# Gate one-hots of a PEER decoder: one comparison for four tokens, products on GpSimd, and a split last write

## The chip, the cores and the metric

The kernel runs on one core of a Trainium2 chip. The metric is the time of one execution in device microseconds; the kernel before took 3640.11 us, the median of three runs (3639.72 to 3644.94).

## What is computed

A decoder trunk of two layers works on 512 tokens of 1024 features. Each layer has a hybrid mixer, a cross-attention and a PEER feed-forward part, each followed by a layer norm. Only the PEER part is touched:

```
v1, i1 = top_k(s1, 16); v2, i2 = top_k(s2, 16)          # per token and head, 128 keys each
sc, ci = top_k(v1[:, None] + v2[None, :], 16)
expert = i1[ci // 16] * 128 + i2[ci % 16]                # 8 heads x 16 = 128 experts per token
gate   = softmax(sc)
act    = gelu(sum_d x[t, d] * u[expert[t, e], d])
out[t] = sum_e gate[t, e] * act[t, e] * v[expert[t, e]]
```

## The kernel before, in words

For tokens 0 to 383 the PEER part is computed densely: all 128 x 128 experts, in 128 chunks of 128. For each chunk `u_chunk` makes the activations of the 384 tokens on TensorE (24 matmuls, lines 230 to 232, three passes of split floats) and `dense` later multiplies them by a gate matrix (`coef`), splits the result and multiplies it with the chunk of v (`v_block`). Tokens 384 to 511 are done by gathering rows of u and v with indirect DMAs on GpSimd's queue (`gathered`, L998), beside the dense part.

The gate matrix of one token is the sum over its 128 choices of gate times one-hot(first key) times one-hot(second key). `gate_rows` makes it as a matmul of two one-hot matrices with the 128 choices on the partitions. For a block of 128 tokens, TensorE transposes the keys and gates into a PSUM bank `pt` (L950, L954), ScalarE copies them to `st` (L951, L955), and then four tokens at a time (a quad) go through:

- VectorE, token by token: `o1 = (iota == key1) * gate` (L964) and `o2 = (iota == key2)` (L968); for three quads of sixteen ScalarE makes `o2` instead (L966, L970);
- TensorE: four matmuls into one bank (L973; the trace shows each as two passes);
- ScalarE: copy of the bank into a stage of 32 tokens (L974), which SP writes to the DRAM tensor `gates` once it is full (L977).

A layer has 3 blocks, 96 quads and 12 writes. The one-hots live in the arena `mid`, whose seven buffers of eight pages hold six quads and the block's columns. The dense part reads `gates` back in pieces of four chunks for all tokens (L1225).

Work is written as generators that are woven together in `body`; a scheduler then sets the order on each engine. Thirty chunks (`AHEAD`) of u are done ahead of the dense part: 20 with the routing, 3 (`EARLY`) at once, some woven into the gates' writing, and the last `LATE` after it. The split of a u chunk in this stage is a cast on ScalarE (L225) and a subtraction on VectorE (L226). DMAs of u, v and gates all go through SP's queue, in order.

Of the kernel before, what the change touches and what calls it, by code (L numbers as in the profile page):

```python
# [10 lines left out]
F32 = mybir.dt.float32  # L11
# [4 lines left out]
AF = mybir.ActivationFunctionType  # L16
OP = mybir.AluOpType
# [7 lines left out]
NK = 128  # L25
# [7 lines left out]
DT = 384  # L33
GT = 32
AHEAD = 30
QUERY = 20
EARLY = 3
LATE = 3
PF = 3
TAIL = 4  # L40
ROWS = 7
# [25 lines left out]
def weave(*streams):  # L67

    live = [[g, 0.0, t] for g, t in streams]
    while live:  # L70
        s = min(live, key=lambda s: s[1] / s[2])
        try:
            s[1] += next(s[0])
        except StopIteration:
            live.remove(s)
# [106 lines left out]
class K:  # L182
# [754 lines left out]
    def gate_rows(self, tb, ga, ef, dram, stages):  # L937

        nc = self.nc
        w = self.al((640,), F32, 1)  # L940
        f12 = w[:, 0:256].rearrange("p (a b) -> p a b", a=2)
        st = w[:, 256:640].rearrange("p (a b) -> p a b", a=3)
        pe = self.bank((128, 4, 128)).bitcast(I32)
        nc.vector.tensor_copy(pe[:, 0], ef[:, tb].rearrange("p h k -> p (h k)"))
        nc.vector.tensor_scalar(pe[:, 1], pe[:, 0], 7, None, op0=OP.logical_shift_right)
        nc.vector.tensor_scalar(pe[:, 2], pe[:, 0], 127, None, op0=OP.bitwise_and)
        nc.vector.tensor_copy(f12, pe[:, 1:3])
        pt = self.bank((128, 3, 128))
        for i in range(2):
            nc.tensor.transpose(pt[:, i, :], f12[:, i], self.ident)  # L950
        nc.scalar.copy(st[:, :2], pt[:, :2])  # L951
        if tb == 0:
            self.softmax(ga.rearrange("p t h k -> p (t h) k"))
        nc.tensor.transpose(pt[:, 2, :], ga[:, tb].rearrange("p h k -> p (h k)"), self.ident)  # L954
        nc.scalar.copy(st[:, 2], pt[:, 2])  # L955
        yield 2
        for g in range(128 // GT):
            stage = stages[:, g % 2]
            for q in range(0, GT, 4):
                t = g * GT + q  # L960
                o1, o2 = (self.al((4, NK), F32, 1) for _ in range(2))
                for k in range(4):
                    c1, c2, cg = (st[:, i, t + k:t + k + 1] for i in range(3))
                    nc.vector.tensor_scalar(o1[:, k], self.iota, c1, cg, op0=OP.is_equal, op1=OP.mult)  # L964
                    if t % 64 in (8, 24, 40):
                        nc.scalar.activation(o2[:, k], self.iota, AF.Abs, scale=-1.0, bias=c2)  # L966
                    else:
                        nc.vector.tensor_scalar(o2[:, k], self.iota, c2, None, op0=OP.is_equal)  # L968
                if t % 64 in (8, 24, 40):
                    nc.scalar.activation(o2, o2, AF.Relu, scale=-1.0, bias=1.0)  # L970
                bk = self.bank((128, 4, NK))
                for k in range(4):
                    nc.tensor.matmul(bk[:, k, :], o2[:, k, :], o1[:, k, :], start=True, stop=True)  # L973
                nc.scalar.copy(stage[:, :, q:q + 4], bk.rearrange("p t e -> p e t"))  # L974
                self.fr(o1, o2)
                yield 1.1
            nc.sync.dma_start(dram[:, tb * (128 // GT) + g], stage)  # L977
        self.fr(w)

    def gathered(self, l, tb, X, peer, gb, out):  # L980
# [98 lines left out]
    def body(self, out):  # L1079
# [19 lines left out]
        for l in range(L):  # L1099
# [15 lines left out]
            self.middle(self.F)  # L1115
            n = AHEAD - peer.c - LATE
            stages = self.al((2, NK, GT))
# [4 lines left out]
            weave(((peer.u_chunk() or 3.9 for _ in range(n - EARLY)), 3.9 * (n - EARLY)), (rows, 110))  # L1122
            for _ in range(LATE):
                peer.u_chunk()
# [247 lines left out]
```

## Time and profile before

| what | value |
|---|---|
| median of three runs | 3640.11 us |
| the profiled execution, its own time | 3637.7 us |
| its span on the core | 3636.0 us |
| TensorE busy | 3512.5 us (97%) |
| VectorE busy | 2694.8 us (74%) |
| ScalarE busy | 1425.0 us (39%) |
| GpSimd busy | 956.2 us (26%) |
| mean DMA rate | 205 GB/s |

Busy time is the time in which at least one instruction of the engine was running, as a share of the span. Matmul rows overlap, so TensorE's share says that it was occupied, not that it ran at its peak. An idle time is put down to the engine whose work ended it. Times in the rows are microseconds from the span's start, means of one instruction are nanoseconds.

### The profile page before, as it was taken

Reading aid. Unit: us, or ns where it says so; the run is one execution under the profiler, and the core shown is the slowest. Engines: PE = TensorE matmul, PEld = TensorE weight load, DVE = VectorE, ACT = ScalarE, POOL = GpSimd, SP = SyncE. Lnnn points to the kernel's source line nnn. Section 1 sums busy time; section 2 is a strip of 40 time slices with the busy share of each in tenths; the row PEclk is TensorE's granted clock in tenths of the full one; section 3 lists DMA queues with packets and bytes.
Section 4 is the critical chain, followed back from the end, with each engine's and each line's share of the span. In section 5 each row is a group of like instructions: output and inputs, shape, how many; then the busy total and the mean of one; then the engine's idle time right before and its main releaser. Section 6 shows DMA issues by size and latency. Waiting matters only on the chain. (4 is left out here: it accounts for less than half of the span.)

```text
span 3636.0 us, 50571 instructions
## 1 busy us (share of the span) xinstructions
PE 3512.5 (97%) x18546; PEld 3054.1 (84%) x18546; DVE 2694.8 (74%) x6206; ACT 1425.0 (39%) x2351; POOL 956.2 (26%) x629
## 2 busy tenths in 40 slices
PE   9999999898999999999999999998999999999998
PEld 6678888777899999998876788887779999999987
DVE  4675469997777777778746755699978777777787
ACT  5553332453333333334345533324533333333342
POOL 0110043002344444445101100430014444443450
PEclk9999999999999999999999999999999999999999
DMA  4142222347988888889612322313479888888894
GB/s 149 58 149 67 91 98 71 111 166 258 319 300 301 296 293 296 301 294 328 235 36 69 126 73 97 101 63 119 160 277 331 286 304 299 301 288 303 296 328 151
DMA packets 280297, 744.47 MB, mean 205 GB/s; under 512 B 21616, under 2 KB 120176, under 8 KB 276976
## 3 DMA queue, kind: packets, MB, share of 16 engines
q1 hardware_dynamic: 206320, 472.76, 37.9%
q0 software_dynamic: 73728, 268.47, 21.2%
q8 instruction: 146, 2.39, 0.3%
q14 instruction: 103, 0.84, 0.1%
HBM read 685.57 MB, written 55.57 MB: 204 GB/s over the span
## 5 line engine op out<-in xcount | busy, mean ns | idle before, releaser
L232 PE MATMUL bk<-parts 128*128 128x384 f32 (+1 forms) x3746 | 1353.7, 361 | 4.5 <-DVE parts L226 4.5
L231 PE MATMUL bk<-parts 128*128 128x384 f32 (+2 forms) x3752 | 1336.5, 356 | 2.6 <-DVE parts L226 2.4
L230 PE MATMUL bk<-parts 128*128 128x512 f32 (+1 forms) x3554 | 1280.1, 360 | 13.7 <-ACT parts L225 13.7
L226 DVE TENSOR_TENSOR parts<-plain,parts 128x1024 fp32r<-128x1024 f32 (+2 forms) x747 | 727.8, 983 | 424.5 <-issue 362.7
L225 ACT CAST parts<-plain 128x1024 fp32r<-128x1024 f32 (+2 forms) x787 | 656.4, 863 | 729.8 <-PE bk L231 636.2
L232 PEld LDWEIGHTS bk<-parts 128*128 128x128 f32 x3746 | 705.5, 188 | 74.7 <-DVE parts L226 7.7
L231 PEld LDWEIGHTS bk<-parts 128*128 128x128 f32 x3752 | 708.2, 189 | 67.6 <-DVE parts L226 3.3
L230 PEld LDWEIGHTS bk<-parts 128*128 128x128 f32 x3554 | 670.7, 189 | 77.1 <-ACT parts L225 14.3
L998 POOL DMA_INDIRECT mid<-peer_u,plain x256 | 372.9, 1457 | 916.2 <-DVE plain L1033 374.0
L998 POOL DMA_INDIRECT mid<-peer_v,plain x256 | 381.2, 1489 | 514.4 <-DVE mid L1021 386.4
L230 PE MATMUL bk<-parts,mid 128*128 128x512 f32 (+2 forms) x912 | 350.3, 387 | 11.2 <-ACT mid L225 7.8
L1215 ACT ACTIVATE plain<-bk 128x384 f32<-128x384 f32 x256 | 125.5, 490 | 582.5 <-PE bk L232 579.5
L1033 DVE SCALAR_TENSOR_TENSOR plain<-mid,plain 128x1024 f32<-128x1024 f32 x256 | 328.8, 1284 | 3.2
L231 PE MATMUL bk<-parts,mid 128*128 128x512 f32 (+2 forms) x912 | 326.6, 359 | 1.5 <-DVE parts L226 1.5
L1021 DVE SCALAR_TENSOR_TENSOR mid<-mid,plain 128x1024 f32<-128x1024 f32 x256 | 303.1, 1219 | 3.0 <-DMA mid<-peer_u,plain 3.0
L973 PE MATMUL bk<-mid 128*128 128x128 f32 x1536 | 282.5, 311 | 13.2 <-DVE mid L964 6.9
L973 PEld LDWEIGHTS bk<-mid 128*128 128x128 f32 x1536 | 219.5, 195 | 75.8 <-DVE mid L968 33.2
L232 PE MATMUL bk<-parts,mid 128*128 128x512 f32 (+2 forms) x720 | 253.1, 353 | 0.0
L964 DVE TENSOR_SCALAR mid<-iota,mid 128x128 f32<-128x128 f32 x768 | 245.8, 341 | 0.3 <-ACT mid L955 0.3
L225 ACT CAST mid<-plain 128x1024 fp32r<-128x1024 f32 x163 | 169.0, 1038 | 193.0 <-PE bk L232 84.7
L226 POOL TENSOR_TENSOR parts<-plain,parts 128x1024 fp32r<-128x1024 f32 x40 | 99.4, 2489 | 524.9 <-ACT parts L225 505.7
L230 PE MATMUL bk<-mid,parts 128*128 128x256 f32 (+1 forms) x798 | 237.0, 297 | 0.0
(237 smaller groups left out, 3834.5 us busy)
## 6 DMA issues: line engine op xcount, KB each, us to landing
plain<-peer_uT SPq DMA_DIRECT2D x256, 512.0 KB
plain<-peer_v SPq DMA_DIRECT2D x256, 512.0 KB
gates<-plain SPq DMA_DIRECT2D x24, 2048.0 KB
plain<-gates SPq DMA_DIRECT2D x64, 768.0 KB
plain<-w_in SPq DMA_DIRECT2D x44, 512.0 KB
plain<-xa_wkv SPq DMA_DIRECT2D x32, 512.0 KB
plain<-peer_wq SPq DMA_DIRECT2D x32, 512.0 KB
plain<-w_out SPq DMA_DIRECT2D x16, 512.0 KB
```

Source lines behind the costliest of these rows:

```text
L225: nc.scalar.copy(hi, src)
L226: return (eng or nc.vector).tensor_sub(lo, src, hi.bitcast(F32))
L230: nc.tensor.matmul(out, lt[0], rt[0], start=first, stop=False)
L231: nc.tensor.matmul(out, lt[0], rt[1], start=False, stop=False)
L232: nc.tensor.matmul(out, lt[1], rt[0], start=False, stop=last)
L964: nc.vector.tensor_scalar(o1[:, k], self.iota, c1, cg, op0=OP.is_equal, op1=OP.mult)
L973: nc.tensor.matmul(bk[:, k, :], o2[:, k, :], o1[:, k, :], start=True, stop=True)
L998: nc.gpsimd.indirect_dma_start(out=t, out_offset=None, in_=self.a[n], in_offset=bass.IndirectOffsetOnAxis(ap=ei[:, s:s + 1], axis=0))
L1021: nc.vector.scalar_tensor_tensor(u, u, 1.0, x, op0=OP.mult, op1=OP.mult, accum_out=act[:, s:s + 1])
L1033: nc.vector.scalar_tensor_tensor(acc, v, act[:, s:s + 1], acc, op0=OP.mult, op1=OP.add)
L1215: k.nc.scalar.activation(g, bk[:, :DT], AF.Gelu)
```

## The change

Per quad, one VectorE instruction compares both key columns, read straight from the PSUM bank `pt` by broadcast, with `iota` and writes both one-hots of four tokens (128 x 1024 elements). GpSimd multiplies the first one-hot by the gates. For two quads of eight ScalarE makes the second one-hot, and VectorE's instruction has 128 x 512 elements. `LATE` goes from 3 to 5. The last write of `gates` in a layer is issued as two: the columns of the first eight chunks, then the rest.

```diff
-LATE = 3
+LATE = 5
...
         for g in range(128 // GT):
             stage = stages[:, g % 2]
             for q in range(0, GT, 4):
                 t = g * GT + q
-                o1, o2 = (self.al((4, NK), F32, 1) for _ in range(2))
-                for k in range(4):
-                    c1, c2, cg = (st[:, i, t + k:t + k + 1] for i in range(3))
-                    nc.vector.tensor_scalar(o1[:, k], self.iota, c1, cg, op0=OP.is_equal, op1=OP.mult)
-                    if t % 64 in (8, 24, 40):
-                        nc.scalar.activation(o2[:, k], self.iota, AF.Abs, scale=-1.0, bias=c2)
-                    else:
-                        nc.vector.tensor_scalar(o2[:, k], self.iota, c2, None, op0=OP.is_equal)
-                if t % 64 in (8, 24, 40):
-                    nc.scalar.activation(o2, o2, AF.Relu, scale=-1.0, bias=1.0)
+                n = 1 if q % 16 == 8 else 2
+                o = self.al((2, 4, NK), F32, 1)
+                sh = [128, n, 4, NK]
+                nc.vector.tensor_tensor(o[:, :n], pt[:, :n, t:t + 4, None].to_broadcast(sh),
+                                        self.iota[:, None, None, :].to_broadcast(sh), op=OP.is_equal)
+                nc.gpsimd.tensor_mul(o[:, 0], o[:, 0], st[:, 2, t:t + 4, None].to_broadcast([128, 4, NK]))
+                if n == 1:
+                    for k in range(4):
+                        nc.scalar.activation(o[:, 1, k], self.iota, AF.Abs, scale=-1.0, bias=st[:, 1, t + k:t + k + 1])
+                    nc.scalar.activation(o[:, 1], o[:, 1], AF.Relu, scale=-1.0, bias=1.0)
                 bk = self.bank((128, 4, NK))
                 for k in range(4):
-                    nc.tensor.matmul(bk[:, k, :], o2[:, k, :], o1[:, k, :], start=True, stop=True)
+                    nc.tensor.matmul(bk[:, k, :], o[:, 1, k, :], o[:, 0, k, :], start=True, stop=True)
                 nc.scalar.copy(stage[:, :, q:q + 4], bk.rearrange("p t e -> p e t"))
-                self.fr(o1, o2)
+                self.fr(o)
                 yield 1.1
-            nc.sync.dma_start(dram[:, tb * (128 // GT) + g], stage)
+            at = tb * (128 // GT) + g
+
+            for a, b in ((0, NK),) if at + 1 < DT // GT else ((0, 8), (8, NK)):
+                nc.sync.dma_start(dram[:, at, a:b], stage[:, a:b])
```

In the changed kernel the compare stands at L965, the product at L967, the matmuls at L974, the copy at L975, the writes at L981, the gathers at L1002 and the reads of gates at L1229.

GpSimd's queue at the end of layer 0's gate stage (the `mid` buffers hold quads or gathered rows), first before:

```order
L226 TENSOR_TENSOR parts<-plain,mid_78 128x1024
L226 TENSOR_TENSOR parts<-plain,parts 128x1024 x7
L998 DMA mid_5556<-peer_u,plain 128x1024
L998 DMA mid_5560<-peer_u,plain 128x1024
L998 DMA mid_5561<-peer_u,plain 128x1024
```

and now:

```order
L967 TENSOR_TENSOR mid_5560<-mid_5560,mid_5562 128x512
L1002 DMA mid_5556<-peer_u,plain 128x1024
L967 TENSOR_TENSOR mid_5561<-mid_5561,mid_5562 128x512
L967 TENSOR_TENSOR mid_5559<-mid_5559,mid_5562 128x512
L1002 DMA mid_5560<-peer_u,plain 128x1024
L967 TENSOR_TENSOR mid_5557<-mid_5557,mid_5562 128x512
L967 TENSOR_TENSOR mid_5558<-mid_5558,mid_5562 128x512
L1002 DMA mid_5561<-peer_u,plain 128x1024
```

The first gather came straight after the last splits of the u chunks; now 96 products stand between, and two gathers stand ahead of the layer's last four and last two products.

SP's queue at the same place, with the queues each instruction waits for (a name with DMAHW is one of eight queues that DMAs take in turn), before:

```order
L977 DMA gates<-plain 128x4096 [waits DMAHW4_49,Activation_49]
L1178 DMA plain<-peer_v 128x1024 [waits DMAHW5_49,DMAHW1_49,DVE_49]
L1178 DMA plain<-peer_uT 128x1024
L1225 DMA plain<-gates 128x12x128 [waits DMAHW7_49,DMAHW4_49]
L1225 DMA plain<-gates 128x12x128
```

and now:

```order
L981 DMA gates<-plain 128x256 [waits DMAHW2_49,Activation_49]
L981 DMA gates<-plain 128x3840
L1182 DMA plain<-peer_v 128x1024 [waits DMAHW4_49]
L1182 DMA plain<-peer_uT 128x1024 [waits DVE_49]
L1229 DMA plain<-gates 128x12x128 [waits DMAHW6_49,DMAHW3_49,DMAHW2_49]
L1229 DMA plain<-gates 128x12x128
```

The small write takes queue 2 and the large one queue 3, and the first read of gates waits for both (queue 6 is its own), where it waited for the one write on queue 4 (queue 7 was its own).

TensorE's queue between two token blocks of layer 0, before:

```order
L973 MATMUL bk<-mid_5561 128x128 x4
L950 MATMUL bk<-ident,mid_5562 128x128 x2
L954 MATMUL bk<-ident,plain 128x128
L973 MATMUL bk<-mid_5557 128x128 x4
L973 MATMUL bk<-mid_5558 128x128 x4
```

and now:

```order
L974 MATMUL bk<-mid_5557 128x128 x4
L974 MATMUL bk<-mid_5558 128x128 x4
L950 MATMUL bk<-ident,mid_5559 128x128 x2
L954 MATMUL bk<-ident,plain 128x128
L974 MATMUL bk<-mid_5560 128x128 x4
L974 MATMUL bk<-mid_5561 128x128 x4
```

In both orders the next block's transposes stand behind all quads of the block before; what changed is what must follow them (a compare, and a product on GpSimd) before the next matmul can start.

## Rows read from the trace of the kernel before

**Rows 1.** The page's busy time, share of the span and instructions by engine.

```profile
PE 3512.5 (97%) x18546; PEld 3054.1 (84%) x18546; DVE 2694.8 (74%) x6206; ACT 1425.0 (39%) x2351; POOL 956.2 (26%) x629
```

**Rows 2.** Busy time by stretch, around the gate stage of layer 0.

```profile
core 0: us, PE busy (x) PEld busy (x) DVE busy (x) ACT busy (x) POOL busy (x), PEclk, DMA share, GB/s
681.10:739.50 58.40, 55.26 (x307) 45.13 (x307) 58.35 (x241) 36.57 (x72) 0.00 (x0) 0.97 0.35 140
853.50:869.40 15.90, 15.87 (x92) 15.55 (x90) 2.86 (x3) 3.87 (x6) 8.64 (x8) 1.00 0.93 350
869.40:878.10 8.70, 0.00 (x0) 0.00 (x0) 1.11 (x3) 0.52 (x2) 0.00 (x0) 0.69 1.11 341
```

**Rows 3.** L973's own view (ns min/median/max), and a row of TensorE's timeline.

```profile
L973 PE MATMUL bk<-mid x1536: 270/275/553, 689.8 to 2668.7; 128*128 128x128 f32 x192
...
726.33 0.38 PE L973 MATMUL bk<-mid 128*128 128x128 f32 x2
```

**Rows 4.** Timeline of VectorE at the start of layer 0's gate stage.

```profile
676.13 3.50 DVE L226 TENSOR_TENSOR parts<-plain,parts 128x1024 fp32r<-128x1024 f32 x3
...
683.01 2.63 DVE L968 TENSOR_SCALAR mid<-iota,mid 128x128 f32<-128x128 f32 x13
...
689.40 0.85 DVE L964 TENSOR_SCALAR mid<-iota,mid 128x128 f32<-128x128 f32 x3
```

**Rows 5.** VectorE by line and shape, 681.1 to 853.5 us: count, busy, mean, idle.

```profile
L964 DVE TENSOR_SCALAR mid<-iota,mid 128x128 f32<-128x128 f32 x384 | 123.6, 344 | 0.2 <-ACT mid L955 0.2
L968 DVE TENSOR_SCALAR mid<-iota,mid 128x128 f32<-128x128 f32 x312 | 86.8, 283 | 2.2 <-ACT mid L951 2.2
```

**Rows 6.** Timeline of TensorE, with its waits, at both layers' gate stages.

```profile
681.11 0.66 PE L950 MATMUL bk<-ident,mid 128*128 128x128 f32 x2 [7.22 <-DVE mid L947]
...
878.14 0.80 PE L230 MATMUL bk<-parts 128*128 128x512 f32 x1 [8.77 <-ACT parts L225]
...
2496.54 0.66 PE L950 MATMUL bk<-ident,mid 128*128 128x128 f32 x2 [7.22 <-DVE mid L947]
...
2689.89 0.79 PE L230 MATMUL bk<-parts 128*128 128x512 f32 x1 [4.92 <-ACT parts L225]
```

**Rows 7.** Timeline of GpSimd, and of VectorE beside it, in layer 0.

```profile
159.93 1.90 POOL L495 TENSOR_TENSOR plain<-plain 128x512 f32<-128x512 f32 x1 [5.45 <-PE bk L230]
...
220.27 1.04 POOL L495 TENSOR_TENSOR plain<-plain 128x512 f32<-128x512 f32 x1 [5.19 <-DVE plain L470]
...
221.05 0.69 DVE L577 SCALAR_TENSOR_TENSOR plain<-bk,plain 128x512 f32<-128x512 f32 x1 [0.85 <-ACT plain L576]
...
479.15 4.75 POOL L226 TENSOR_TENSOR mid<-plain,mid 128x1024 fp32r<-128x1024 f32 x2 [10.93 <-ACT mid L225]
```

**Rows 8.** GpSimd by line and shape, whole span.

```profile
L639 POOL TENSOR_TENSOR plain<-plain 128x512 f32<-128x512 f32 x4 | 5.1, 1285 | 2.0 <-DVE plain L638 2.0
```

**Rows 9.** ScalarE by line and shape, 681.1 to 853.5 us.

```profile
L974 ACT COPY plain<-bk 128x512 f32<-128x512 f32 x96 | 55.9, 585 | 56.6 <-PE bk L973 55.9
L966 ACT ACTIVATE mid<-iota,mid 128x128 f32<-128x128 f32 x72 | 27.1, 399 | 2.1 <-PE bk L973 1.6
```

**Rows 10.** Timeline of TensorE and ScalarE between the first two token blocks, layer 0.

```profile
741.33 0.41 PE L950 MATMUL bk<-ident,mid 128*128 128x128 f32 x2 [2.00 <-DVE mid L947]
...
741.78 0.37 ACT L951 COPY mid<-bk 128x256 f32<-128x256 f32 x1 [1.82 <-PE bk L950]
```

**Rows 11.** Timeline of GpSimd: the first gathers of layer 0 and layer 1.

```profile
845.20 9.71 POOL L998 DMA_INDIRECT mid<-peer_u,plain  x1 [200.29 <-PE bk L973]
...
2660.49 1.00 POOL L998 DMA_INDIRECT mid<-peer_u,plain  x1 [199.96 <-ACT plain L974]
```

**Rows 12.** Timeline of SP's queue and VectorE: last gates write, gates back.

```profile
854.04 0.33 SPq L977 DMA_DIRECT2D gates<-plain  x1
...
876.99 1.49 DVE L1236 TENSOR_TENSOR plain<-plain 128x384 f32<-128x384 f32 x3 [14.79 <-DMA plain<-gates]
...
2670.24 0.33 SPq L977 DMA_DIRECT2D gates<-plain  x1
```

## The prediction

> **What bounds the kernel now.** I read the page's busy shares first, then the stretches of the first layer, then VectorE, GpSimd and the queue waits inside the stretch that the change touches. Over the whole span TensorE is busy 97% [rows 1], so only a stage in which TensorE is not the pace can gain. The gate stage is one: from the first transposes of L950 to the last gate column it fills 172 us of layer 0, and in its first third VectorE is busy 58.35 of 58.40 us [rows 2]. TensorE's 55.26 us there are overstated, since matmul rows overlap: two passes of L973 together take 0.38 us where the median of one is 0.275 [rows 3], so they follow each other every 0.11 us, and the eight passes of four tokens need about 0.89 us. VectorE needs more. One L964 starts every 0.26 us (three in 0.85 us) and one L968 every 0.20 us (thirteen in 2.63 us) [rows 4], so four tokens cost 4 x 0.26 + 4 x 0.20 = 1.8 us. With 384 L964 and 312 L968 in the layer [rows 5] that is 162 us. The stage is VectorE's.
>
> Behind it TensorE runs late u chunks for 15.9 us (92 matmuls, 0.173 us each, so 4.15 us for a chunk of 24) and then stands still, in layer 0 for 8.77 us and in layer 1 for 4.92 us, until the first gates are back from DRAM and split [rows 2, 6]. From L950 to the first dense matmul it is 681.11 to 878.14 = 197.0 us in layer 0 and 2496.54 to 2689.89 = 193.4 us in layer 1 [rows 6]. The sum replaces these two stretches; the rest of the program keeps its order.
>
> **The change, part by part.** *Compares.* Four tokens now take one VectorE instruction of 128x1024 (72 of 96 quads a layer) or 128x512 (24 quads). No row shows this form. The nearest are three 128x1024 subtractions in 3.50 us, one every 1.17 us [rows 4], and a 128x512 with a PSUM operand at 0.69 us [rows 7], which starts the next about 0.6 us on. That gives 72 x 1.17 + 24 x 0.6 = 99 us a layer in place of 162, a mean of 1.0 us per quad. Bounds: 0.9 (the PSUM side no dearer) to 1.2 (every wait exposed); both stay under the next item, so neither is priced.
>
> *Products.* Each quad adds one GpSimd multiply of 128x512 with two different operands. The row of that kind is 1.285 us (L639) [rows 8]; two queued 128x1024 instructions with two operands took 4.75 us [rows 7], 2.375 each or 1.19 for each half. Between 1.19 and 1.285, near the row of the right size, I take one product every **1.25 us**. Bounds: 1.04 us, what GpSimd takes where both operands are one tensor [rows 7], and 1.90 us, what the same instruction took beside a VectorE subtraction with two SBUF operands [rows 7]. I stay at 1.25: the compare has one operand in PSUM, and beside such an instruction (L577, 0.69 us, from 221.05) GpSimd kept its 1.04 us [rows 7]. So GpSimd, at 1.25, becomes the pace, over VectorE at 1.0 and TensorE at 0.89.
>
> On elementwise work a rule speaks against this. The rows say 1.285 us on GpSimd against 0.69 us on VectorE. The Trainium skill, GPSIMD Engine Reference, section Engine selection, gives elementwise multiplies to VectorE because GpSimd is about twice as slow with two inputs; the ratio of these rows agrees. By that rule the product would stay on VectorE, a quad would cost 1.0 + 0.6 = 1.6 us there, and the result would be 3584 + 2 x 96 x 0.35 = 3651 us. The sum goes by the slower of two engines that work side by side, which the rule does not weigh.
>
> *ScalarE.* It forms 24 instead of 18 quads of the second one-hot. Its copies and absolute values were 55.9 + 27.1 us a layer [rows 9]; 6 x 4 more of 0.40 us add 10, and the closing passes stay small beside that. It stays under the 120 us that GpSimd needs, and works up to six buffers ahead: nothing.
>
> *Block boundaries.* The 32 quads of a token block end before the next block's transposes on TensorE, in both orders. Now three engines stand behind each other there: the last quad 0.95, transposes and wait 0.7, ScalarE's copy (0.37 us [rows 10]) with its hand-over 0.4, a compare 1.2: 3.3 us without a product, twice a layer, 6.6 us. TensorE's gap at that place in the kernel before was 2.00 us [rows 10], which is the lower bound; 5 us each is the upper.
>
> *Gathers on GpSimd's queue.* The first gathers now stand between the last six products: one ahead of four products, one ahead of two. The first gather of the program took 9.71 us; the first of layer 1 took 1.00 [rows 11], and with some 0.3 us to the next instruction I count 1.25 for an ordinary one. In the old order nothing waited for it. I charge 9.71 + 0.3 + 1.25 = 11.3 us in layer 0 and 2.5 us in layer 1. Bounds: 2.5 us, if the 9.71 does not come back, and 14 us.
>
> *Lead-in.* Before, the first L964 starts 8.3 us after L950 (689.40 [rows 4]). The split L226 now stands ahead of L852, and the first product needs a compare (1.2 us) behind L852: 8.8 us.
>
> *LATE 5.* Two chunks move out of the stage, where GpSimd's pace leaves TensorE idle anyway, to behind it. Six chunks then follow the last gate: 24.9 us. The gates' own path, from the issue of the last write to the first dense matmul, was 854.04 to 878.14 = 24.1 us in layer 0 (VectorE gets the gates at 876.99) and 19.7 us in layer 1 [rows 6, 12]; one more microsecond lies between the last pass and that issue. So 25.1 us in layer 0, 24.9 in layer 1: both standstills go, paid with 8.3 us of chunks each.
>
> *The write split in two.* In the built order the first gates read waits for two write queues, the small write's and the large one's, where it waited for one. So it comes no earlier: nothing, at best 0.2 us in layer 0.
>
> **Sum.** Layer 0: 8.8 lead-in + 96 x 1.25 = 120.0 + 6.6 + 11.3 + 1.1 (last quad) + 25.1 = 172.9 us against 197.0. Layer 1: 8.8 + 120.0 + 6.6 + 2.5 + 1.1 + 24.9 = 163.9 against 193.4. Saved: 24.1 + 29.5 = 53.6 us. The profiled execution's own time is 3637.7 us (span 3636.0), 2.4 us under the median 3640.1 of the runs shown; 3637.7 - 53.6 = **3584 us**.
>
> **The rivals.** *VectorE and GpSimd take turns* (slower). If the compare kept GpSimd from its operands as L226 did, a quad would cost 1.17 + 1.25 us (72 of them) or 0.6 + 1.25 (24), 2.28 on average, 99 us more per layer: 3584 + 198 = 3782. It decides from a pitch of 1.5 us, where the stage eats what it saves. For it: the 1.90 us row; against it: 1.04 us beside a PSUM operand [rows 7]. The Trainium skill, SBUF — State Buffer, section Who interferes with whom, states the lock between the two engines and excepts VectorE instructions with at most one SBUF input; the rows just named agree with both halves. Chance 0.07.
>
> *Products at 1.40 us*, by the broadcast operand or the hand-overs, which no row shows: 2 x 96 x 0.15 = 29 us, 3613. Chance 0.15.
>
> *Products near 1.04 us*: then the mean pace falls to about 1.08, where VectorE and TensorE hold it: 33 us less, 3551. Chance 0.10.
>
> *The DMA engines set the dense start.* They are at 0.93 and more behind the stage [rows 2], and gathers, gate writes, reads, v and u loads still meet there; 10 us a layer would give 3604. Against it: no u chunk needed there is loaded there, since the order has all of them issued in the stage. Chance 0.10.
>
> *The change does not do what it says*: for the split of the write it is already so in the sum.
>
> **How the numbers follow.** The forecast, at 0.58, has its own spread of some 10 us (boundary, first gather). The range, 3556 to 3614, holds it, the backlog and the 1.40 case, and leaves out the turn-taking (0.07), most of the fast products (0.07) and a tail beyond 1.40 (0.05). A measurement of this kernel tells a change from none at about 0.2%, 7 us. Only the turn-taking and mishaps beyond a pitch of 1.5 end slower: faster 0.92, same 0.02, slower 0.06.
>
> **What would show it.** In the profile of the changed kernel: GpSimd's multiply at about 1.28 us and one every 1.25; VectorE's compare at 1.2 us with idle time behind GpSimd; a GpSimd row of nearly 10 us among the last products of layer 0 alone, with TensorE idle beside it; GpSimd pauses of about 3 us at two places a layer; no wait of several microseconds before the first dense matmul. Wrong would be multiplies of 1.6 us and more, compares of 2 us, or TensorE still standing before the dense part.

## The result, and the profile after

The changed kernel took 3532.7 us (median of four runs) beside 3642.5 us for the kernel before: a ratio of 0.9704, 95% interval 0.9682 to 0.9727. It is faster, as forecast, by twice as much as forecast: the prediction was 3584, its range ended at 3556. The profiled execution's own time is 3532.14 us, its span 3530.4; all differences below are of spans, 3636.0 to 3530.4 = 105.6 us.

The page's busy times after, against [rows 1]:

```profile
PE 3417.4 (97%) x18546; PEld 3022.8 (86%) x18546; DVE 2570.0 (73%) x5006; ACT 1431.2 (41%) x2411; POOL 1136.0 (32%) x821
```

TensorE runs the same 18546 matmuls in 95 us less of occupied time, at the same 97%. The share says nothing; where TensorE was held by others, it is held for less.

The two new lines' own views (ns min/median/max; first and last start), where [rows 7, 8] had given the bounds:

```profile
L967 POOL TENSOR_TENSOR mid<-mid,mid x192: 1036/1039/1048, 692.4 to 2560.7; 128x512 f32<-128x512 f32 x192
...
L965 DVE TENSOR_TENSOR mid<-bk,iota x192: 674/1215/1225, 691.1 to 2555.8; 128x1024 f32<-128x1024 f32 x144, 128x512 f32<-128x512 f32 x48
```

The compare is as expected. The product is not: 1.04 us each time, none longer than 1.048, where 1.28 was expected.

GpSimd's timeline through layer 0's gate stage (start, duration of the merged row, count, and in brackets the idle time before it with what ended it), against [rows 11]:

```profile
692.39 32.11 POOL L967 TENSOR_TENSOR mid<-mid,mid 128x512 f32<-128x512 f32 x32 [46.42 <-DVE mid L965]
728.70 1.04 POOL L967 TENSOR_TENSOR mid<-mid,mid 128x512 f32<-128x512 f32 x1 [4.20 <-DVE mid L965]
729.89 22.00 POOL L967 TENSOR_TENSOR mid<-mid,mid 128x512 f32<-128x512 f32 x22 [0.16 <-DVE mid L965]
754.19 9.29 POOL L967 TENSOR_TENSOR mid<-mid,mid 128x512 f32<-128x512 f32 x9 [2.30 <-DVE mid L965]
767.69 1.04 POOL L967 TENSOR_TENSOR mid<-mid,mid 128x512 f32<-128x512 f32 x1 [4.21 <-DVE mid L965]
768.89 26.98 POOL L967 TENSOR_TENSOR mid<-mid,mid 128x512 f32<-128x512 f32 x27 [0.16 <-DVE mid L965]
797.04 1.11 POOL L1002 DMA_INDIRECT mid<-peer_u,plain  x1 [1.17 <-ACT plain L975]
798.18 2.04 POOL L967 TENSOR_TENSOR mid<-mid,mid 128x512 f32<-128x512 f32 x2
800.38 0.97 POOL L1002 DMA_INDIRECT mid<-peer_u,plain  x1 [0.16 <-POOL mid L967]
801.38 2.04 POOL L967 TENSOR_TENSOR mid<-mid,mid 128x512 f32<-128x512 f32 x2
```

GpSimd has no gap between its products: 32 of them in 32.11 us, a pause of 4.2 us at each block boundary, one of 2.30 us behind the one u chunk that is still woven in, and two gathers of about 1 us between the last products. All 96 products take 96.5 us.

VectorE has no gap between its compares either. Its timeline over the first block, and at the woven chunk:

```profile
691.09 32.03 DVE L965 TENSOR_TENSOR mid<-bk,iota 128x1024 f32<-128x1024 f32 x32 [0.78 <-ACT mid L955]
...
751.17 1.80 DVE L226 TENSOR_TENSOR parts<-plain,parts 128x1024 fp32r<-128x1024 f32 x1 [0.86 <-PE bk L231]
```

The next compare starts 1.13 us behind the start of a full one and 0.60 us behind that of a half one (128x512): one starts at 692.23 and, four quads later, one at 696.22. That is 1.00 us a quad, as on GpSimd: the two engines set the pace together.

TensorE's timeline at the same places, against [rows 6, 10], and the gates' return, against [rows 12]:

```profile
693.49 0.79 PE L974 MATMUL bk<-mid 128*128 128x128 f32 x2 [2.73 <-POOL mid L967]
...
729.79 4.55 PE L974 MATMUL bk<-mid 128*128 128x128 f32 x22 [2.80 <-POOL mid L967]
...
2440.73 0.66 PE L950 MATMUL bk<-ident,mid 128*128 128x128 f32 x2 [7.22 <-DVE mid L947]
...
2587.74 0.39 PE L230 MATMUL bk<-parts 128*128 128x512 f32 x1
```

```profile
805.33 0.80 SPq L981 DMA_DIRECT2D gates<-plain  x2
817.44 2.92 SPq L1229 DMA_DIRECT2D plain<-gates  x2
825.89 1.03 DVE L1240 TENSOR_TENSOR plain<-plain 128x384 f32<-128x384 f32 x2 [7.56 <-DMA plain<-gates]
```

The first dense matmul (L230, 128x512) of layer 1 starts with no wait before it, at 2587.74; in layer 0 it does so at 829.50. From L950 to it: 681.92 to 829.50 = 147.6 us in layer 0, and 147.0 in layer 1. That is 49.4 and 46.4 us less than [rows 6] give. Of the rest of the 105.6 us, 7.2 lie between the dense start of layer 0 and layer 1's L950 and 3.4 behind the dense start of layer 1; 0.8 us was lost ahead of layer 0's L950.

### The profile page after: what moved, and what is told of

Same layout as the page of the kernel before. It is cut to its first block, busy times and chain, and to the rows that moved or that the text cites. A ratio compares the mean times of both kernels' runs of the same rounds, so it can differ in the third digit from the quotient of the medians.

```text
span 3530.4 us, 49767 instructions
## 1 busy us (share of the span) xinstructions
PE 3417.4 (97%) x18546; PEld 3022.8 (86%) x18546; DVE 2570.0 (73%) x5006; ACT 1431.2 (41%) x2411; POOL 1136.0 (32%) x821
## 4 chain that ended last, share of the span: by engine, by line
PE 81%; DVE 12%; issue 3%; ACT 2%; POOL 1%; DMA 1%; DVEq 0%; SPq 0%; POOLq 0%; ACTq 0%
PE bk L230 24%; PE bk L231 23%; PE bk L232 23%; PE bk L974 5%; DVE bk L866 2%; DVE bk L860 1%; DVE plain L862 1%; PE bk L771 1%; DVE parts L226 1%; PE bk L742 1%; PE bk L572 1%; PE bk L528 1%; DVE plain L327 1%; DVE plain L858 1%; DVE plain L864 1%
## 5 line engine op out<-in xcount | busy, mean ns | idle before, releaser
L230 PE MATMUL bk<-parts 128*128 128x512 f32 (+1 forms) x3554 | 1276.1, 359 | 0.7 <-ACT parts L225 0.7
L226 DVE TENSOR_TENSOR parts<-plain,parts 128x1024 fp32r<-128x1024 f32 (+2 forms) x747 | 730.0, 985 | 445.4 <-issue 363.9
L230 PEld LDWEIGHTS bk<-parts 128*128 128x128 f32 x3554 | 669.0, 188 | 63.4 <-ACT parts L225 1.1
L1002 POOL DMA_INDIRECT mid<-peer_v,plain x256 | 377.4, 1474 | 494.4 <-DVE mid L1025 377.4
L1002 POOL DMA_INDIRECT mid<-peer_u,plain x256 | 363.9, 1421 | 530.6 <-DVE plain L1037 378.7
L230 PE MATMUL bk<-parts,mid 128*128 128x512 f32 (+2 forms) x912 | 349.5, 386 | 11.1 <-ACT mid L225 7.6
L226 POOL TENSOR_TENSOR parts<-plain,parts 128x1024 fp32r<-128x1024 f32 x40 | 99.4, 2490 | 526.6 <-ACT parts L225 507.8
L230 PE MATMUL bk<-mid,parts 128*128 128x256 f32 (+1 forms) x798 | 237.0, 297 | 0.0
L967 POOL TENSOR_TENSOR mid<-mid,mid 128x512 f32<-128x512 f32 x192 | 192.6, 1040 | 115.6 <-DVE mid L965 114.8
L232 PE MATMUL bk<-mid,parts 128*128 128x256 f32 (+1 forms) x798 | 228.9, 287 | 0.0
L230 PEld LDWEIGHTS bk<-parts,mid 128*128 128x128 f32 (+1 forms) x912 | 171.8, 189 | 56.6 <-issue 17.8
```

Source lines behind the costliest of these rows:

```text
L226: return (eng or nc.vector).tensor_sub(lo, src, hi.bitcast(F32))
L230: nc.tensor.matmul(out, lt[0], rt[0], start=first, stop=False)
L232: nc.tensor.matmul(out, lt[1], rt[0], start=False, stop=last)
L967: nc.gpsimd.tensor_mul(o[:, 0], o[:, 0], st[:, 2, t:t + 4, None].to_broadcast([128, 4, NK]))
L1002: nc.gpsimd.indirect_dma_start(out=t, out_offset=None, in_=self.a[n], in_offset=bass.IndirectOffsetOnAxis(ap=ei[:, s:s + 1], axis=0))
```

## The experiments

**1. What makes the product cheap.** Edit, against the changed kernel:

```diff
-nc.gpsimd.tensor_mul(o[:, 0], o[:, 0], st[:, 2, t:t + 4, None].to_broadcast([128, 4, NK]))
+nc.gpsimd.tensor_mul(o[:, 0], o[:, 0], w[:, 128:640].rearrange("p (a b) -> p a b", a=4))
```

> Only the second operand of GpSimd's product differs: 512 separate elements per partition (the block's key and gate columns as they lie) in place of the four gate columns broadcast. The gates are therefore not applied; the work and its order stay. Theory: the broadcast operand is what makes the product take 1.04 us and start every 1.01. Then it takes about 1.28 us here and starts every 1.25, as the row with two full operands had it, and the time rises by up to 2 x 96 x 0.24 = 46 us, to 3565 to 3580. Rival: a product written over its own first operand takes 1.04 us with any second one; then nothing changes, 3533 within 7 us.

Measured: 3578.9 us, ratio 0.9803 (0.9787 to 0.982) to the kernel before. The product's own view and GpSimd's first row:

```profile
L967 POOL TENSOR_TENSOR mid<-mid,mid x192: 1254/1278/1324, 692.2 to 2608.2; 128x512 f32<-128x512 f32 x192
...
692.21 39.50 POOL L967 TENSOR_TENSOR mid<-mid,mid 128x512 f32<-128x512 f32 x32 [46.39 <-DVE mid L965]
```

32 products in 39.50 us are one every 1.23. Same shape, same count, same order, same in-place output: only the second operand has 512 elements of its own instead of 4 that are repeated. That is worth 46 us here. The time comes close to the 3584 us forecast for such products, partly by chance, since the forecast's other misses nearly cancel (see below).

**2. Do compare and product hold each other off?** The compare reads the copy in SBUF:

```diff
-nc.vector.tensor_tensor(o[:, :n], pt[:, :n, t:t + 4, None].to_broadcast(sh),
+nc.vector.tensor_tensor(o[:, :n], st[:, :n, t:t + 4, None].to_broadcast(sh),
```

> The compare reads the key columns from their copy in SBUF in place of the PSUM bank; the result is the same. Theory (the rival of the prediction, which took turns as the slower case): with two SBUF operands the compare and GpSimd's product keep each other off, a quad costs 1.17 + 1.01 us (72 of 96) or 0.6 + 1.01 (24), mean 2.04, and a layer's stage grows from 111 to about 200 us: 3533 + 2 x 85 = 3700 or more, with compares or products of 2 us. Rival: the two engines do not disturb each other at these sizes; compare 1.2 us, product 1.04 us, 3533 within 10 us.

Measured: 3677.3 us, ratio 1.007 (1.0053 to 1.0087): 0.7% slower than the kernel before. The views of the two lines:

```profile
L967 POOL TENSOR_TENSOR mid<-mid,mid x192: 1032/2015/2019, 691.5 to 2703.1; 128x512 f32<-128x512 f32 x192
...
L965 DVE TENSOR_TENSOR mid<-mid,iota x192: 678/2054/4617, 682.1 to 2697.8; 128x1024 f32<-128x1024 f32 x144, 128x512 f32<-128x512 f32 x48
```

Both lines' medians rise to 2.0 us; the stage from first to last gate column grows from 111.2 to 180.4 us. The rival of the prediction exists, and what keeps the change clear of it is that the key columns are read from PSUM. It cost 145 us, not the 198 forecast for it: a quad takes 180.4 / 96 = 1.88 us, and with the product's real 1.0 us even full turn-taking would be 2.04. The Trainium skill, SBUF — State Buffer, section Who interferes with whom, says that a VectorE instruction with two SBUF inputs contends with a GpSimd instruction that reads SBUF, and one with a single SBUF input does not; these two kernels agree with both halves (2.02 against 1.04 us). In the kernel before, the GpSimd multiply of 1.90 us in [rows 7] stood beside two such instructions on VectorE:

```profile
159.72 1.22 DVE L226 TENSOR_TENSOR mid<-plain,mid 128x1024 fp32r<-128x1024 f32 x1
160.85 2.06 DVE L226 TENSOR_TENSOR parts<-plain,mid 128x1024 fp32r<-128x1024 f32 x1
```

**3. The products on VectorE.**

```diff
-nc.gpsimd.tensor_mul(o[:, 0], o[:, 0], st[:, 2, t:t + 4, None].to_broadcast([128, 4, NK]))
+nc.vector.tensor_mul(o[:, 0], o[:, 0], st[:, 2, t:t + 4, None].to_broadcast([128, 4, NK]))
```

> The products are done on VectorE, all else as in the changed kernel. Theory: VectorE sets the pace alone, 72 x (1.17 + 0.6) + 24 x (0.6 + 0.6) = 156 us a layer against 111 now: 3533 + 2 x 45 = 3620 to 3645. Rival: GpSimd's hand-overs cost as much as they save, and the time stays within 20 us of 3533. GpSimd has nothing to do here for about 150 us before the first gather of layer 0: if that idleness is why the first gather took 9.71 us in the kernel before, it takes 9 us or more here; if not, about 1.1 us.

Measured: 3645.3 us, ratio 0.9992 (0.998 to 1.0003). GpSimd's first gather in layer 0:

```profile
846.61 1.11 POOL L1002 DMA_INDIRECT mid<-peer_u,plain  x1 [201.49 <-PE bk L974]
```

So the one-instruction compare without GpSimd's help (but with `LATE` = 5 and the split write) brings nothing that can be measured; nearly the whole gain is that the product runs on a second engine. A product takes 0.676 us on VectorE and 1.04 on GpSimd. By the Trainium skill, GPSIMD Engine Reference, section Engine selection, elementwise work belongs on VectorE; engine by engine these rows agree, and the kernel that follows it is 113 us slower than the one that doesn't, because VectorE was the pace and GpSimd idle.

**4. The first gather's 9.71 us.** The kernel before once more, without an edit:

> The kernel before, once more, for one row of its profile: the first gather of layer 0 on GpSimd, 9.71 us in the profile that the prediction read. If that is a price of this place in the program (GpSimd idle for 200 us, DMA engines full), it is 9 us or more again; if it was an event of that one execution, it is 1 to 1.5 us, as with LATE = 5 alone (1.44) and with the products on VectorE (1.11), where GpSimd had been idle just as long.

Measured: 3651.4 us (one run). GpSimd's rows (layer 0, layer 1), and VectorE's beside the second:

```profile
844.99 9.70 POOL L998 DMA_INDIRECT mid<-peer_u,plain  x1 [200.40 <-PE bk L973]
...
2663.48 9.70 POOL L998 DMA_INDIRECT mid<-peer_u,plain  x1 [199.94 <-ACT plain L974]
```

```profile
2670.80 0.40 DVE L968 TENSOR_SCALAR mid<-iota,mid 128x128 f32<-128x128 f32 x1
2670.99 1.34 DVE L226 TENSOR_TENSOR parts<-plain,parts 128x1024 fp32r<-128x1024 f32 x1
2675.23 1.23 DVE L226 TENSOR_TENSOR parts<-plain,parts 128x1024 fp32r<-128x1024 f32 x1 [2.90 <-issue]
```

It came back, now in both layers, so it is no accident of one execution; and experiment 3 shows that it is not the idle time either. What the long gathers share is their end. VectorE's uninterrupted run of one-hots and a split, all on SBUF, ends at 2672.33, and the gather at 2673.18. In layer 0 it is 853.70 and 854.69 here, 853.91 and 854.91 in the trace of before. That suggests that the gather's issue is held until VectorE pauses. To test it, VectorE's compares and products were given nothing but SBUF operands (edits of experiments 2 and 3 together), and GpSimd no products:

> The changed kernel with the products on VectorE and the compare reading its columns from SBUF, so that VectorE runs instructions with two SBUF operands without a pause while the first gather of layer 0 is issued on GpSimd, idle for some 150 us before. Theory: the 9.7 us gathers of the kernel before were held until VectorE's run of instructions on SBUF ended (in all three, the end lies 0.9 to 1.0 us behind the end of that run); here too the first gathers are held or stretched: at least one row of 1.5 us or more, perhaps as long as the rest of VectorE's run. Rival: only the kernel before's short instructions, or its place, do that; 1.0 to 1.2 us as with the products on VectorE and the compare from PSUM. The time itself: 3640 to 3650 by either.

Measured: 3630.8 us (one run), below the 3640 to 3650 expected; why it is shorter than experiment 3 stays open. GpSimd in layer 0 and layer 1, and VectorE in layer 0:

```profile
840.96 5.82 POOL L1002 DMA_INDIRECT mid<-peer_u,plain  x1 [196.55 <-PE bk L974]
...
2648.83 5.82 POOL L1002 DMA_INDIRECT mid<-peer_u,plain  x1 [195.75 <-ACT plain L975]
```

```profile
844.50 1.28 DVE L967 TENSOR_TENSOR mid<-mid,mid 128x512 f32<-128x512 f32 x2
851.40 1.23 DVE L226 TENSOR_TENSOR parts<-plain,parts 128x1024 fp32r<-128x1024 f32 x1 [5.62 <-PE bk L231]
```

VectorE's run ends at 844.50 + 1.28 = 845.78; the gather ends at 846.78, a normal gather's 1.0 us later, and the next takes 0.94. With the compare reading PSUM (experiment 3, otherwise the same work) it takes 1.11. In both layers of all nine traces here whose compare reads PSUM the first gather took 0.97 to 1.12 us. So a gather's issue can wait for the end of a whole run of VectorE instructions on SBUF. It does not always: the six first gathers beside the old one-hots took 9.71 and 1.00 us in the trace of before [rows 11], 9.70 twice in the run above, and 1.44 and 1.00 with `LATE` = 5 alone (experiment 5). What decides between the two stays open, and two held gathers in experiment 4 against none in experiment 3 make the operands the likely cause, not a certain one.

The same section of the Trainium skill says that a DMA issued from GpSimd stalls beside VectorE when GpSimd can't get at the shared ports to generate its descriptors; the long gathers agree with that. It puts this down to VectorE's two-port modes and says that `tensor_tensor` did not stall a DMA; beside the gather of 5.82 us VectorE ran `tensor_tensor` instructions alone, so there the runs differ from it.

Whether the gather is held also goes with the dense start: with 9.70 us in layer 1 TensorE stood still for 9.00 us there, with 1.00 us for 4.92 [rows 6]. The 8.77 and 4.92 us of the two layers in [rows 6] thus go with the gather's length, not with the layer.

**5. LATE.** Five instead of three in the kernel before, and three instead of five in the changed kernel.

> The kernel before with LATE = 5 alone. Theory A: the gates' own path (24 us from the last write to the first dense matmul) sets the dense start in both; the two chunks leave the stage, which shortens by the 2 to 3 us of their splits on VectorE and little else, so 5 to 8 us in both layers together: 3633 to 3638. Theory B: the standstill of 8.77 and 4.92 us also costs what follows it, since TensorE's first matmuls of the dense part start every 0.43 us where later ones start every 0.23; with the standstills gone another 5 to 10 us come back behind the dense start, and the time is 3620 to 3632. The first gather of layer 0 is 9 us or more if GpSimd's long idleness causes it (it stays idle here).

Measured: 3641.1 us, ratio 0.9979 (0.9969 to 0.9989): 6.7 us below the kernel before as it was run beside it (3647.8), the amount of theory A, though above both theories' ranges. The standstills are gone, but the dense part starts hardly earlier: 877.80 in layer 0 against 878.14. Chunks fill the wait, and the stage, with VectorE as its pace, is hardly shorter without them (162.4 us from first to last gate column, 163.6 before). Theory B is half right: the first ten matmuls behind the dense start take 2.31 us instead of 4.44, and then waits for L226, the longest 1.56 us, take that back.

> The changed kernel with LATE back at 3: two u chunks go back into the gate stage. Theory of the prediction: GpSimd's pace leaves TensorE idle in the stage, the two chunks cost nothing there; behind the last gate four chunks (16.6 us) run, and TensorE then stands still until the gates are back, 21 to 23 us behind the last gate instead of 24.8: dense starts 2 to 3 us earlier per layer, 3527 to 3533. Rival: a woven chunk costs the stage most of its own time (in the changed kernel the block with one chunk took 34.7 us, the one without 32.0), so 2 x 2.7 us per layer more in the stage, less 2 to 3 before the dense part, and a slow start of TensorE behind a standstill of 4 to 6 us: 3536 to 3545.

Measured: 3550.1 us, ratio 0.9727 (0.9711 to 0.9743), 17 us above the changed kernel and 5 us above the rival's range. TensorE's row at the dense start of layer 0 (the wait is 6.21 us in layer 1), and the stretch behind it (columns: PE, PEld, DVE, ACT and POOL busy time, then PEclk, the granted clock as a share of full speed, DMA share and GB/s):

```profile
832.48 0.79 PE L230 MATMUL bk<-parts 128*128 128x512 f32 x1 [4.81 <-ACT parts L225]
```

```profile
832.48:836.80 4.32, 4.32 (x10) 3.26 (x11) 4.32 (x9) 1.75 (x3) 0.00 (x0) 0.51 0.96 300
```

The changed kernel's row for the same matmuls:

```profile
829.50:831.80 2.30, 2.30 (x11) 1.89 (x11) 2.30 (x6) 1.43 (x2) 0.00 (x0) 1.00 1.01 392
```

In the gate stage the two chunks cost 6.4 us in layer 0 (117.6 us from first to last gate column instead of 111.2) and 7.5 in layer 1 (118.5 instead of 111.0): over 3 us each of their own 4.15. Some 5 us of that come back, since the dense part follows the last gate by 21.5 and 22.9 us instead of 24.8, and some 8 are lost behind the two dense starts. Behind a standstill TensorE starts at a granted clock of 0.51, the lower level of 1.2 GHz, and loses 2 us of these each time. The prediction took the chunks in the stage to be free; they are not: in the changed kernel's stage of 111.2 us TensorE is busy 101.9, GpSimd 98.3, VectorE 97.9 and ScalarE 93.2. VectorE's compares run without a gap, so a chunk's split (1.80 us behind a wait of 0.86 in the result's rows) delays them, and GpSimd stands 2.30 us behind it.

**6. The split of the last write.** One write again:

```diff
-for a, b in ((0, NK),) if at + 1 < DT // GT else ((0, 8), (8, NK)):
-    nc.sync.dma_start(dram[:, at, a:b], stage[:, a:b])
+nc.sync.dma_start(dram[:, at], stage)
```

> The changed kernel with the last gates write in one piece again. Prediction: the first read waits for both pieces anyway, so nothing changes, and whatever the path of the gates gains or loses, up to 2 us, is covered by the six u chunks: within 4 us of the changed kernel. Rival: the large write of the last block's columns is on the path to the dense start and the split lets it start sooner; then the gates are back 2 us or more later here, TensorE waits before the dense part, and the time is 5 us or more above the changed kernel.

Measured: 3532.9 us against 3532.7 (ratio 0.9677, 0.9661 to 0.9692). The kernel before took 3642.5 us beside the changed kernel and 3652.7 beside this one, so these ratios differ by the base alone. As predicted, nothing: the read is issued at 816.03 here and at 817.44 with the split.

**7. The boundary pauses.** The next block's columns are made early (the first half of `gate_rows` as a function of its own, its result handed on):

```diff
                 self.fr(o)
+                if t == 100 and tb + 1 < DT // 128:
+                    held.append(self.gate_cols(tb + 1, ga, ef))
                 yield 1.1
```

> The changed kernel with the columns of the next token block (conversion, transposes, copies) made after the 26th quad of a block instead of behind its last. Theory: at each of the two block boundaries of a layer GpSimd stands 4.2 us for a hand-over through four engines; with the columns ready it goes on within 1 us, the columns' 1.8 us on VectorE hide beside products, and 2.5 to 3.2 us are saved at four places: 3520 to 3523. Rival: VectorE (98 of 111 us busy) is as near its limit as GpSimd, its instructions between the compares push GpSimd back by as much, and a second buffer for columns takes one from the quads: 3530 or more.

Measured: 3530.0 us, ratio 0.9669 (0.9653 to 0.9685): 3 us below the changed kernel, less than a measurement of it can tell, and not the 3520 to 3523 of the theory. VectorE at the second boundary, and GpSimd:

```profile
762.82 3.67 DVE L971 TENSOR_TENSOR mid<-bk,iota 128x1024 f32<-128x1024 f32 x3 [2.86 <-PE bk L980]
...
764.12 1.04 POOL L973 TENSOR_TENSOR mid<-mid,mid 128x512 f32<-128x512 f32 x1 [3.51 <-DVE mid L971]
```

It came out as the rival had it: the hand-over through four engines is gone, but GpSimd still stands 3.51 us (4.21 in the changed kernel), and VectorE now waits 2.86 us for TensorE, most likely for a buffer of one-hots, since the early columns hold one of the seven.

**8. The lead-in.** VectorE's rows ahead of layer 0's columns in the changed kernel:

```profile
676.95 3.50 DVE L226 TENSOR_TENSOR parts<-plain,parts 128x1024 fp32r<-128x1024 f32 x3
680.36 0.29 DVE L944 CAST bk<-plain 128x128 int32<-128x128 f32 x1
```

Three splits of u chunks stand ahead of the key conversions, while TensorE waits 7.22 us for these and GpSimd has nothing for 46 us. On top of experiment 7 they were moved, with the changed kernel run beside them:

```diff
-self.split(self.uq, c + 1, k.nc.gpsimd if c + 1 < QUERY else None)
+self.split(self.uq, c + 1, k.nc.gpsimd if c + 1 < QUERY + EARLY + 5 else None)
```

> The changed kernel once more, as the base for the two versions beside it on the same chip: 3530 to 3536.

> Early columns, and in addition four of the five splits of u chunks (L226) that stand on VectorE between the last top-k and the first compare go to GpSimd, which is idle there for 46 us. One split stays on VectorE ahead of L852. Theory: the three splits ahead of the key conversions (3.50 us) hold up the columns and with them TensorE's L950, which waits 7.2 us; the lead-in gets 3.5 to 4.7 us shorter in both layers, 3530 - 7 to 10 = 3520 to 3524. Rival: a split takes about 2.4 us on GpSimd, the u chunks there come later, and TensorE waits for them instead: 3530 or more.

> As before it, with the fifth split on GpSimd too. Theory: it waits for a buffer that TensorE frees at about 688 us and then keeps GpSimd 2.4 us, to within a microsecond of the first product, so it neither wins nor loses against the version with one split left on VectorE: within 3 us of it. Rival: it blocks GpSimd ahead of the products and gives back 2 us or more per layer.

Measured: 3533.3, 3524.7 (+ 4 in place of + 5) and 3518.1 us, ratios 0.9686 (0.9671 to 0.97), 0.966 (0.9646 to 0.9675) and 0.9635 (0.9621 to 0.9648). TensorE and GpSimd with all five moved:

```profile
682.04 0.59 PE L950 MATMUL bk<-ident,mid 128*128 128x128 f32 x2 [3.95 <-DVE bk L847]
...
691.67 0.60 PE L980 MATMUL bk<-mid 128*128 128x128 f32 x3 [3.36 <-POOL mid L973]
```

```profile
688.26 2.36 POOL L226 TENSOR_TENSOR parts<-plain,parts 128x1024 fp32r<-128x1024 f32 x1 [7.77 <-PE bk L232]
690.57 10.03 POOL L973 TENSOR_TENSOR mid<-mid,mid 128x512 f32<-128x512 f32 x10
```

L950's wait falls from 7.22 to 3.95 us. The last split waits for TensorE and ends just as the first product can start. From TensorE's last matmul ahead of L950 to the first product it is 12.5 us, 17.7 in the changed kernel. L950 itself starts no earlier in this execution, 682.04 against 681.92, but at 675.25 in the profile with four splits moved; what sets the two apart ahead of the stage stays open. This version is 15 us below the changed kernel and has the lowest median of the study. Its runs (3515.4 to 3523.6) and those with four splits moved (3515.7 to 3530.7) overlap, so whether the 6.6 us between the medians, more than the 3 expected, are real stays open too.

## Why the prediction was wrong

The direction and the mechanism were right, the pace-setter only half; two terms were too high. Layer 0, forecast and measured:

| term | forecast | measured |
|---|---|---|
| lead-in, L950 to first product | 8.8 | 10.5 |
| 96 products | 120.0 | 96.5 |
| two block boundaries | 6.6 | 8.4 |
| pause behind the woven chunk, hand-overs | 0 | 2.6 |
| gathers between the last products | 11.3 | 3.5 |
| last quad | 1.1 | 1.3 |
| last gate to first dense matmul | 25.1 | 24.8 |
| sum | 172.9 | 147.6 |

- **Products (the step that failed).** "One product every 1.25 us" was taken from L639, the row "of the right size" with two full operands. The operand here is four values repeated, and with it the product costs what [rows 7] show where both operands are one tensor: 1.04 us, one every 1.0. Experiment 1 shows it: 1.28 us with a full operand, and 3578.9 us. Both layers: 23.5 and, by the same rows of layer 1, 23.2 make 47 us of the 51 us that the forecast was off. That this one term makes up nearly all of it is partly chance: 7.8 us of the gather and 9.8 us outside the two stretches nearly cancel against some 12 us of terms that were too cheap. The case "near 1.04" had a chance of 0.10 and a pace of 1.08, on the ground that VectorE and TensorE would hold it there. VectorE does hold it, but at 1.00: 72 full compares at 1.13 and 24 half ones at 0.60 make 0.998 us a quad, with no gap. So GpSimd is not the pace over VectorE, as the prediction had it; the two tie. By these rows a cheaper product alone would win little more, and what is put between the compares lengthens the stage (experiments 5 and 7).
- **First gather.** "I charge 9.71 + 0.3" carried over a duration without its cause. Most likely VectorE's one-hots on SBUF held the gather, as they did in some executions and not in others (experiment 4). In the changed kernel the compare reads PSUM, and the gather takes 1.11 us: 7.8 us too much in the forecast.
- **Lead-in, boundaries and the woven chunk** were 1.7, 1.8 and 2.6 us too cheap in layer 0 and took back part of the two.
- **Standstills** went as forecast: the dense part follows the last gate by 24.8 us in both layers, within 0.3 us of the forecast, without a wait, which is the time of the six u chunks. So the DMA engines, a rival of the prediction, did not set the dense start. Not priced was what lies behind them. Together 10.6 us came back there; the low clock at the dense start explains 2.1 us of it in each layer. The rest were waits for L226 among the first dense chunks (2.4 us in layer 0) and small ones later; they also occur in kernels without a standstill (experiment 5), and their cause stays open.
- **Turn-taking**, the rival on the other side, was rightly put off by the PSUM operand (experiment 2), on thin evidence: the multiply of 1.04 us from 220.27 and L577 from 221.05 [rows 7] overlap by 0.26 us only. Products at 1.40 us, the other slower case, did not come: none took over 1.048 us. **The write's split** was rightly put at nothing (experiment 6). The rival that put the product on VectorE was priced at 3651, and the run gave 3645.3.
- **LATE 5** was right in the sum, for a partly wrong reason: its two chunks were not free in the stage, where VectorE had no slack for their splits (experiment 5). In the kernel before it is worth 0.2%, in the changed one 17 us.

## What to carry to other kernels

Price an instruction from a row with the same kind of operands, not only the same shape: how an operand is laid out (full or repeated, in PSUM or SBUF) decided 46 and 145 us here. A long duration in a trace is only a price once it is known what held it; look at what the neighbouring engine was doing at its end. And when an engine sets the pace of a stage, moving work to a slower, idle one can win, as long as the two don't hold each other off, as they did with the compare reading SBUF.

## What was not expected of the hardware

GpSimd's 128x512 multiply takes 1.04 us with a second operand of four repeated values and 1.28 us with one of 512. Five first gathers on GpSimd took 4.8 to 8.7 us beyond their usual 1.0 and ended 0.9 to 1.0 us behind a run of VectorE instructions on SBUF with no pause, so they seem to have been held across instruction boundaries, while GpSimd's multiplies, in experiment 2, got through between two compares. Three other gathers beside the same one-hots were not held.
